# Each SwiGLU of a two-layer encoder in two halves of its columns, each half with its own part of the down projection

## The chip, the cores and the metric

The kernel runs on one core of one Trainium2 chip. The metric is the device time of one execution in microseconds (us); the median of several runs is compared. Engines are PE (matmuls), PEld (its weight loads), DVE, ACT, POOL and SP (which issues the DMAs).

## The reference, cut to what matters

The input is 256 tokens of width 1024. Two layers each add a SwiGLU, a mixer and another SwiGLU to the running sum x, each on RMS-normalised x. The mixer of layer 0 is grouped attention, that of layer 1 neighbourhood attention; the change does not touch them.

```
def swiglu(h, w_gate, w_up, w_down):
    return (jax.nn.silu(h @ w_gate) * (h @ w_up)) @ w_down
...
    for layer in range(DEPTH):
        i = layer // 2
        h = rms_norm(x, ffn1_norm[layer])
        x = x + 0.5 * swiglu(h, ffn1_w_gate[layer], ffn1_w_up[layer], ffn1_w_down[layer])
        h = rms_norm(x, mix_norm[layer])
...
        h = rms_norm(x, ffn2_norm[layer])
        x = x + 0.5 * swiglu(h, ffn2_w_gate[layer], ffn2_w_up[layer], ffn2_w_down[layer])
    return rms_norm(x, final_norm)
```

The inner width D_FF is 2816, that is 22 blocks of 128 rows of w_down, or 11 pairs of blocks. All data is float32.

## The kernel before

**Stages.** The program runs six stages in a row: SwiGLU (stage 0), even mixer (1), SwiGLU (2), SwiGLU (3), odd mixer (4), SwiGLU (5). x lies in two tiles of 128 tokens, `x0` and `x1`.

**Products.** Each float32 operand is split into a high and a low part: ACT copies the high part (`high_part`, tiles `hi`), DVE subtracts it to get the low part (`low_part`, tiles `lo`). A product is three matmuls (`mm`, lines 407 to 409): high by high, low by high, high by low. Weights arrive by DMA in raw tiles of 1 MB (three buffers, `RAWS`), are split into pieces of 512 columns, two pieces to a split of 1024, and wait in seven buffers (`FIT["wp"]`). One piece serves both token tiles, so six matmuls.

**A SwiGLU stage (`ffn`).** The 2816 columns of gate and up are done in six chunks (`FF_CHUNKS`). For each chunk the gate of both token tiles is accumulated in two s banks of PSUM, then the up part in two pj banks; ACT applies silu, DVE multiplies (`glu`), PE transposes the product, and it is split again (tiles `g`). After all six chunks comes the down projection over the 11 pairs of blocks. `DOWN` lists for each stage in which order, and how: `p` is a plain pair (two blocks, two token tiles, two halves of the output: eight products), `s` a Strassen pair. A Strassen pair (`seven`) needs seven products instead of eight, and for it DVE forms sums of the weights (line 338) and of the activations (`quarters`, `sums_of`), which are split too (tiles `shi`, `slo`; `FIT["sum"]` buffers).

**Banks.** PSUM has eight banks, handed out by tags in turn: three s, two pj, one o, two tp. A down uses all of them: four for the output `Y`, four for the Strassen sums `M`.

**End of a stage.** Once the last Strassen pair is issued, `combine` adds the four sums `M` into x (one ACT copy, line 713, and eight DVE operations, lines 710 to 728). The last two pairs of the list (`HELD`) are held back and run output half by output half, so that each half of x can be added (`add_to_x`, line 537) while PE goes on. Then PE transposes x for the next stage (`prepare`, line 462), ACT and DVE split it (lines 447 and 452).

**Order.** Every engine runs its instructions in the order in which the program writes them. The code decides that order with a clock of its own: each product calls `tick`, which moves the waiting tasks (the generators) one step on, and supplies the next split when the rate set for the place (`RATE`, `DOWN_RATE`, `ENDS`) makes it due.

Of the kernel before, what the change touches and what calls it, by code (L numbers as in the profile page):

```python
# [30 lines left out]
FF_CHUNKS = [512, 512, 512, 512, 384, 384]  # L31
# [17 lines left out]
HELD = 2  # L49
# [106 lines left out]
def pairs(stage):  # L156
    return [({"p": "plain", "s": "strassen"}[o[0]], int(o[1:])) for o in DOWN[stage].split()]
# [9 lines left out]
class Trunk:  # L167
# [4 lines left out]
    def __init__(self, ctx, tc, a, out):  # L172
        self.ctx, self.tc, self.nc, self.a, self.out = ctx, tc, tc.nc, a, out
        pool = lambda name, bufs, **kw: ctx.enter_context(tc.tile_pool(name=name, bufs=bufs, **kw))
        self.one = pool("one", 1)
        self.ph = None
        self.raw = pool("raw", RAWS)
        self.wp = pool("wp", FIT["wp"])

        self.two = pool("two", 2)  # L180
        self.acc = pool("acc", 1, space=PSUM)
        self.n = 0
        self.rate = RATE[0]
# [69 lines left out]
    def plan(self):  # L253
# [288 lines left out]
    def first_gates(self, W):  # L542
# [26 lines left out]
        self.due = -AHEAD_START * RATE[0]  # L569
# [11 lines left out]
    def ffn(self):  # L581
        nc = self.nc
        self.rate = RATE[self.now.n]

        gT = [{}, {}]
        down = pairs(self.now.n)
        tasks = []

        paired = {2 * pair: [] for kind, pair in down if kind == "strassen"}
        sums = {}  # L590

# [4 lines left out]
        def glu(tt, f0, w, u, s):  # L596
# [7 lines left out]
            pairs = [f for f in range(f0, f0 + n) if f in paired and f + 1 < f0 + n]  # L604
            parts = []
            for f in pairs:
                yield from quarters(tt, f, tb, f - f0)

            if tt == 1 and f0 + n - 2 in pairs:
# [4 lines left out]
            for f in pairs if tt == 1 else []:  # L614
                yield from sums_of(f)

        def quarters(tt, f, tb, at):

            block = lambda i: tb[:, (at + i) * P : (at + i + 1) * P]
            if tt == 0:  # L620
                paired[f] = self.t([P, 4, P], "quarters")
# [10 lines left out]
        def sums_of(f):  # L632
# [5 lines left out]
            hi, lo = (self.t([P, 4, P], f"k{f}{p}", 1, F32R) for p in "hl")  # L638
# [6 lines left out]
        for ci, w in enumerate(FF_CHUNKS):  # L645
            G = self.take(KD)
            S = []
            if self.now.n + ci == 0:
                both = self.first_gates(G)
            for tt in range(NT):  # L650
                g = both[tt] if self.now.n + ci == 0 else self.project(self.ready(tt), G, "s")
                S.append(self.t([P, 512], "silu", 2))
                self.start(silu(tt, w, g, S[tt]))
            U = self.take(KD)
            for tt in range(NT):
                u = self.project(self.now.hT[tt], U, "pj")
                tasks.append(self.start(glu(tt, f0, w, u, S[tt])))
            f0 += w // P
# [3 lines left out]
        if self.next.n == 6:  # L662
# [3 lines left out]
        Y = [[self.bank(("o", "pj")[i] if tt == 0 else "s") for i in range(2)] for tt in range(NT)]  # L666
# [13 lines left out]
        M = {}  # L680

        def seven(pair, first, last):
            b11, b21, b22, t7, t5, t8, t6 = self.take(7)
            if first:
                for task in tasks:
                    self.finish(task)
                self.rate = DOWN_RATE[self.now.n]
# [4 lines left out]
            def temp(name, tag, lh, piece):  # L692
                if first:
# [53 lines left out]
        if self.next.n == 6:
            last = [self.t([P, 2, 512], "shi", FIT["sum"], F32R) for _ in range(NT)]
            self.last = [t.bitcast(F32).rearrange("p a w -> p (a w)") for t in last]
        held = [f for _, pair in down[-HELD:] for f in (2 * pair, 2 * pair + 1)]  # L750
        for f in held:
            W[f] = self.take(2)
        for tt in range(NT):
            for sl in parts[tt]:
# [4 lines left out]
                self.start(self.add_to_x(tt, sl, Y[tt][sl.start // 512] if to is None else to, 0.5))  # L759
# [564 lines left out]
```

## Time and profile before

| | |
|---|---|
| three runs | 965.45, 966.27, 966.73 us (median 966.27) |
| the profiled execution: its time, its span | 965.2 us, 963.4 us |
| PE, DVE, ACT, POOL busy | 99%, 72%, 58%, 9% of the span |
| mean granted PE clock | 0.998 of full speed |
| bytes moved by DMA | 171.64 MB, 178 GB/s on average |

The span reaches from the first to the last instruction; the profiled execution's own time is 1.8 us longer. Busy times overlap, so their sum is more than the span. PE's ends are modelled, so its busy share says that it had work, not how fast it did it.

### The profile page before, as it was taken

How to read it: one execution, taken by the hardware profiler on the slowest of the kernel's cores; microseconds unless marked ns; L12 is line 12 of the kernel's file. 1: busy time of each engine (PE TensorE's matmuls, PEld its weight loads, DVE VectorE, ACT ScalarE, POOL GpSimd, SP SyncE). 2: the span in 40 equal slices, each digit the busy share in tenths (PEclk: the TensorE clock that was granted, in tenths of full speed). 3: DMA queues.
4: the chain of work that ended last, by engine and by line, in shares of the span. 5: the costliest groups of instructions: out<-in, count | busy, mean ns of one | idle time of the engine just before them, and what ended most of it. 6: DMA issues, size and time to landing. Idle time of an engine off the chain costs nothing.

```text
span 963.4 us, 12838 instructions
## 1 busy us (share of the span) xinstructions
PE 950.2 (99%) x4803; PEld 803.6 (83%) x4803; DVE 696.2 (72%) x1104; ACT 557.4 (58%) x965; POOL 87.5 (9%) x152
## 2 busy tenths in 40 slices
PE   9999999999999999999999999999999999999997
PEld 6888998877878888988888899888878888889886
DVE  6665679778866655797865558789877676656987
ACT  7554556477776555565554455547877576545551
POOL 1020000063410000000000000005130000000002
PEclk9999999999999999999999999999999999999999
DMA  8565555644426744666456556564624366545651
GB/s 293 196 237 177 184 209 180 214 132 100 120 88 212 226 153 133 239 219 218 143 195 205 172 156 231 194 227 134 197 101 146 118 206 196 195 147 175 220 172 67
DMA packets 82367, 171.64 MB, mean 178 GB/s; under 512 B 3712, under 2 KB 25216, under 8 KB 82304
## 3 DMA queue, kind: packets, MB, share of 16 engines
q1 hardware_dynamic: 81728, 170.23, 53.5%
q8 instruction: 37, 0.61, 0.3%
q10 hardware_dynamic: 576, 0.59, 0.2%
q14 instruction: 26, 0.21, 0.1%
HBM read 169.76 MB, written 1.05 MB: 177 GB/s over the span
## 4 chain that ended last, share of the span: by engine, by line
PE 91%; DVE 4%; ACT 2%; POOL 1%; issue 1%; DMA 1%; POOLq 0%; ACTq 0%; DVEq 0%
PE pj L407 14%; PE pj L409 14%; PE pj L408 14%; PE s L407 12%; PE s L409 12%; PE s L408 11%; PE tp L484 3%; PE o L815 2%; PE o L409 1%; PE o L407 1%; PE o L408 1%; PE tp L894 1%; DVE lo L418 1%; PE tp L462 1%; PE s L830 1%
## 5 line engine op out<-in xcount | busy, mean ns | idle before, releaser
L418 DVE TENSOR_TENSOR lo<-raw,hi 128x1024 fp32r<-128x1024 f32 (+2 forms) x388 | 383.7, 1012 | 122.0 <-ACT hi L415 118.5
L415 ACT ACTIVATE hi<-raw 128x1024 fp32r<-128x1024 f32 (+2 forms) x388 | 328.1, 878 | 151.0 <-PE pj L409 101.6
L407 PE MATMUL pj<-hi,th 128*128 128x512 f32 (+1 forms) x512 | 198.1, 387 | 0.0
L409 PE MATMUL pj<-hi,tl 128*128 128x512 f32 (+1 forms) x512 | 192.9, 377 | 0.0
L408 PE MATMUL pj<-lo,th 128*128 128x512 f32 (+1 forms) x512 | 192.7, 376 | 0.1
L407 PE MATMUL s<-hi,th 128*128 128x512 f32 (+1 forms) x400 | 152.1, 380 | 0.0
L409 PE MATMUL s<-hi,tl 128*128 128x512 f32 (+1 forms) x400 | 149.1, 373 | 0.0
L408 PE MATMUL s<-lo,th 128*128 128x512 f32 (+1 forms) x400 | 148.9, 372 | 0.0
L409 PEld LDWEIGHTS pj<-hi,tl 128*128 128x128 f32 x512 | 96.1, 188 | 15.5
L407 PEld LDWEIGHTS pj<-hi,th 128*128 128x128 f32 x512 | 96.4, 188 | 13.8 <-issue 0.9
L408 PEld LDWEIGHTS pj<-lo,th 128*128 128x128 f32 x512 | 96.4, 188 | 13.4 <-DVE lo L418 0.5
L409 PEld LDWEIGHTS s<-hi,tl 128*128 128x128 f32 x400 | 75.2, 188 | 11.0
L408 PEld LDWEIGHTS s<-lo,th 128*128 128x128 f32 x400 | 75.3, 188 | 10.3
L407 PEld LDWEIGHTS s<-hi,th 128*128 128x128 f32 x400 | 75.3, 188 | 10.1
L599 DVE SCALAR_TENSOR_TENSOR glu<-pj,rstd,silu 128x512 f32<-128x512 f32 (+1 forms) x48 | 33.6, 701 | 36.8 <-PE pj L409 36.6
L418 DVE TENSOR_TENSOR g_l<-tp,g_h 128x384 fp32r<-128x384 f32 (+1 forms) x48 | 29.0, 604 | 21.8 <-ACT g_h L415 21.8
L427 POOL TENSOR_TENSOR rstd<-var,mhalf 128x1 f32<-128x1 f32 (+2 forms) x16 | 15.2, 948 | 311.0 <-DVE var L425 310.9
L407 PE MATMUL s<-hi,g_h 128*128 128x512 f32 (+1 forms) x108 | 42.8, 396 | 0.0
L415 ACT ACTIVATE g_h<-tp 128x384 fp32r<-128x384 f32 (+1 forms) x48 | 25.2, 526 | 29.1 <-PE tp L484 19.0
L409 PE MATMUL s<-hi,g_l 128*128 128x512 f32 (+1 forms) x108 | 42.0, 389 | 0.0
L408 PE MATMUL s<-lo,g_h 128*128 128x512 f32 (+1 forms) x108 | 41.9, 388 | 0.0
L447 ACT ACTIVATE th<-tp,mats 128x128 fp32r<-128x128 f32 x88 | 25.1, 371 | 28.3 <-PE tp L462 26.1
(378 smaller groups left out, 1380.7 us busy)
## 6 DMA issues: line engine op xcount, KB each, us to landing
raw<-in_ffn_w_down SPq DMA_DIRECT2D x44, 1024.0 KB, 5.1
raw<-in_ffn_w_up SPq DMA_DIRECT2D x32, 1024.0 KB, 5.4
raw<-in_ffn_w_gate SPq DMA_DIRECT2D x30, 1024.0 KB, 5.2
raw<-in_ffn_w_gate SPq DMA_DIRECT2D x16, 768.0 KB, 4.4
raw<-in_ffn_w_up SPq DMA_DIRECT2D x16, 768.0 KB, 4.6
raw<-in_odd_w_qkv SPq DMA_DIRECT2D x12, 1024.0 KB, 5.4
raw<-in_even_w_in SPq DMA_DIRECT2D x4, 1024.0 KB, 5.2
raw<-in_even_w_out SPq DMA_DIRECT2D x8, 512.0 KB, 5.7
```

What stands on the lines that cost most here:

```text
L407: mm(ps, h, wh, start=first, stop=False)
L408: mm(ps, h, wl, start=False, stop=False)
L409: mm(ps, l, wh, start=False, stop=last)
L415: self.nc.scalar.activation(hi, src, AF.Copy)
L418: self.nc.vector.tensor_tensor(lo, src, hi.bitcast(F32), op=ALU.subtract)
L427: nc.gpsimd.tensor_tensor(r[:, :n], v[:, :n], self.mhalf[:, :n], op=ALU.pow)
L447: self.nc.scalar.activation(hi, tb[:, j * P : j * P + P], AF.Copy, scale=gain)
L462: nc.tensor.transpose(tb[:, j * P : (j + 1) * P], self.x[tt][:, b * P : (b + 1) * P], self.ident)
L484: self.nc.tensor.transpose(tb[:, i * P : (i + 1) * P], src[:, i * P : (i + 1) * P], self.ident)
L599: nc.vector.scalar_tensor_tensor(m[:, :w], u[:, :w], self.now.r[tt], s[:, :w], op0=ALU.mult, op1=ALU.mult)
L815: self.nc.tensor.matmul(O[64 * s : 64 * s + 64, i * P : i * P + P], v(b0 + i, s, kc), pT[s][:, i, kc, :], start=(kc == 0), stop=(kc == 1),)
L830: nc.tensor.matmul(S[:, i, :], q, kz[s], start=True, stop=False)
```

## The change

The six chunks are put into two halves (`HALVES`) of three. Each half does gate and up of its three chunks and then its part of the down projection: pairs 0 to 5 in the first half, 6 to 10 in the second. The down projection becomes a method of its own (`down`) that runs twice per stage, each time with a combine and with adds into x; only the second starts the work for the next stage. One pair is held in the first half, two in the second. The sets of `DOWN` are written anew, with 14 letters s in place of 17. The buffers of the Strassen splits go from three to five, the tiles `g` are shared by both halves, and output and sums change the tags of their banks. The rates are written anew.

```diff
-FF_CHUNKS = [512, 512, 512, 512, 384, 384]
...
+HALVES = [[512, 512, 512], [512, 384, 384]]
...
-    0: "p0 s1 p2 s3 p4 s5 p6 s7 p8 p9 p10",
-    2: "p0 s1 p2 s3 p5 p4 s7 p10 s8 p6 p9",
-    3: "p0 s1 p2 s3 s5 p4 p7 p10 s8 p6 p9",
-    5: "p0 s1 p2 s3 s5 p4 s7 s8 p10 p6 p9",
+    0: ["p1 p3 s2 s5 p0 p4", "p6 s7 p8 p10 p9"],
+    2: ["p0 p2 s1 s5 p4 p3", "p6 s7 s8 p10 p9"],
+    3: ["p0 s1 p2 s5 p4 p3", "p6 s7 s8 p10 p9"],
+    5: ["p1 p2 s5 p4 p3 p0", "p6 s7 s8 p10 p9"],
...
-FIT = {"wp": 7, "sum": 3}
+FIT = {"wp": 7, "sum": 5}
...
-RATE = {0: 0.58, 2: 0.58, 3: 0.53, 5: 0.63}
-DOWN_RATE = {0: 1.22, 2: 1.2, 3: 1.2, 5: 1.2}
-ENDS = {0: [0.42, 0], 2: [0.3, 1], 3: [0.35, 0], 5: [0.4, 0]}
+RATE = {0: [0.55, 0.75], 2: [0.65, 0.47], 3: [0.6, 0.5], 5: [0.6, 0.47]}
+DOWN_RATE = {0: [1.18, 1.2], 2: [1.25, 1.1], 3: [1.2, 1.2], 5: [1.3, 1.2]}
+ENDS = {0: [[0.4, 0], [0.4, 0]], 2: [[0.38, 3], [0.4, 0]], 3: [[0.38, -1], [0.4, -1]], 5: [[0.48, 0], [0.4, -1]]}
...
-HELD = 2
+HELD = [1, 2]
...
-            for w in FF_CHUNKS:
-                first = stage == 0 and c0 == 0
-                yield from columns(a[n + "_w_gate"][l], [(c0, w)], FIRST if first else None, "narrow" if first else "wide")
-                yield from columns(a[n + "_w_up"][l], [(c0, w)], None, "wide")
-                c0 += w
-            for i, (kind, pair) in enumerate(pairs(stage)):
-                src = a[n + "_w_down"][l][2 * pair * P : 2 * (pair + 1) * P, :].rearrange("(k p) n -> p k n", p=P)
-                uses = [2, 3 if stage == 5 and i >= len(pairs(stage)) - HELD else 2]
-                yield [(slice(0, P), src)], 2, D, uses, "wide" if kind == "plain" else kind
+            for half, chunks in enumerate(HALVES):
+                for w in chunks:
...
+                    yield from columns(
+                        a[n + "_w_gate"][l], [(c0, w)], FIRST if first else None, "narrow" if first else "wide"
+                    )
+                    yield from columns(a[n + "_w_up"][l], [(c0, w)], None, "wide")
+                    c0 += w
+                down = pairs(stage, half)
+                for i, (kind, pair) in enumerate(down):
+                    src = a[n + "_w_down"][l][2 * pair * P : 2 * (pair + 1) * P, :].rearrange("(k p) n -> p k n", p=P)
+                    uses = [2, 3 if stage == 5 and half == 1 and i >= len(down) - HELD[half] else 2]
+                    yield [(slice(0, P), src)], 2, D, uses, "wide" if kind == "plain" else kind
...
+    def split_psum(self, tb, n, tag, dest, fit=None):
+        hi, lo = (self.t([P, fit or n, P], f"{tag}{p}", 1, F32R)[:, :n, :] for p in "hl")
         flat = lambda t: t.rearrange("p a b -> p (a b)")
...
-        if nxt.n < 6:
+        if nxt.n < 6 or not last:
             yield 1
         x = self.x[tt][:, sl.start : sl.start + ps.shape[-1]]
         self.nc.vector.scalar_tensor_tensor(x, ps, scale, x, op0=ALU.mult, op1=ALU.add)
...
-        self.rate = RATE[self.now.n]
...
-            yield from self.split_psum(tb, n, f"g{tt}_{f0}_", parts)
+            yield from self.split_psum(tb, n, f"g{tt}_{ci}_", parts, 4)
...
         f0 = 0
-        for ci, w in enumerate(FF_CHUNKS):
-            G = self.take(KD)
-            S = []
-            if self.now.n + ci == 0:
-                both = self.first_gates(G)
-            for tt in range(NT):
-                g = both[tt] if self.now.n + ci == 0 else self.project(self.ready(tt), G, "s")
-                S.append(self.t([P, 512], "silu", 2))
-                self.start(silu(tt, w, g, S[tt]))
...
+        for half, chunks in enumerate(HALVES):
+            self.rate = RATE[self.now.n][half]
+            for ci, w in enumerate(chunks):
+                G = self.take(KD)
+                S = []
+                if self.now.n + f0 == 0:
+                    both = self.first_gates(G)
+                for tt in range(NT):
+                    g = both[tt] if self.now.n + f0 == 0 else self.project(self.ready(tt), G, "s")
+                    S.append(self.t([P, 512], "silu", 2))
+                    self.start(silu(tt, w, g, S[tt]))
+                U = self.take(KD)
+                for tt in range(NT):
+                    u = self.project(self.now.hT[tt], U, "pj")
+                    tasks.append(self.start(glu(tt, ci, f0, w, u, S[tt])))
+                f0 += w // P
+            self.down(half, gT, sums, tasks)
+
+    def down(self, half, gT, sums, tasks):
...
+        down, kept = pairs(self.now.n, half), HELD[half]
...
+        end = self.next.n == 6 and half == 1
         W = {}
 
         parts = [[slice(0, 512), slice(512, 1024)] for _ in range(NT)]
-        if self.next.n == 6:
+        if end:
...
-        Y = [[self.bank(("o", "pj")[i] if tt == 0 else "s") for i in range(2)] for tt in range(NT)]
+        M = {"5": self.bank("s")}
+        Y = [[self.bank("s" if tt == 0 else ("o", "pj")[i]) for i in range(2)] for tt in range(NT)]
...
             def temp(name, tag, lh, piece):
-                if first:
+                if name not in M:
                     M[name] = self.bank(tag)
                 self.mm(M[name], lh, piece, first, last)
...
-        for i, (kind, pair) in enumerate(down[:-HELD]):
+        for i, (kind, pair) in enumerate(down[:-kept]):
             if kind == "strassen":
                 seven(pair, i == order[0], i == order[-1])
                 if i == order[-1]:
                     self.start(combine())
-                    self.rate, self.due = ENDS[self.now.n]
+                    self.rate, self.due = ENDS[self.now.n][half]
                 continue
...
-        held = [f for _, pair in down[-HELD:] for f in (2 * pair, 2 * pair + 1)]
+        held = [f for _, pair in down[-kept:] for f in (2 * pair, 2 * pair + 1)]
         for f in held:
             W[f] = self.take(2)
...
                 for f in held:
                     use(f, tt, sl, f == held[-1], to)
-                self.start(self.add_to_x(tt, sl, Y[tt][sl.start // 512] if to is None else to, 0.5))
+                self.start(self.add_to_x(tt, sl, Y[tt][sl.start // 512] if to is None else to, 0.5, half == 1))
```

On PE the old order has 4371 rows and the new one 4380; on DVE 1061 and 1081, on ACT 829 and 818, on SP 192 and 192.

The first place is in stage 0 on PE, at the end of chunk 2's up and the start of chunk 3's gate. Before, the up (pj_762) is followed at once by the gate of the next chunk (s_811):

```order
L407 MATMUL pj_762<-hi_707,th_265 128x512
L408 MATMUL pj_762<-lo_708,th_265 128x512
L409 MATMUL pj_762<-hi_707,tl_266 128x512
L407 MATMUL s_811<-hi_728,th_120 128x512
L408 MATMUL s_811<-lo_729,th_120 128x512
L409 MATMUL s_811<-hi_728,tl_121 128x512
```

Now the last matmuls of the first half's down (pj_810, fourth part of the output) stand ahead of that gate, which is called s_1067:

```order
L412 MATMUL pj_810<-hi_960,g_2_h_852 128x512
L413 MATMUL pj_810<-lo_961,g_2_h_852 128x512
L414 MATMUL pj_810<-hi_960,g_2_l_853 128x512
L412 MATMUL s_1067<-hi_969,th_120 128x512
L413 MATMUL s_1067<-lo_970,th_120 128x512
L414 MATMUL s_1067<-hi_969,tl_121 128x512
```

The whole first down (pairs p1 p3 s2 s5 p0 p4) has moved between chunk 2 and chunk 3. The new gate's bank is the one that held the Strassen sum s_806.

The second place is the same point on DVE. Before, there are only splits of weights (lo) and the products of gate and up (glu):

```order
L418 TENSOR_TENSOR lo_729<-raw_528,hi_728 128x1024
L418 TENSOR_TENSOR lo_742<-raw_528,hi_741 128x1024
L418 TENSOR_TENSOR lo_760<-raw_562,hi_759 128x1024
L599 SCALAR_TENSOR_TENSOR glu_767<-pj_721,rstd_239,silu_676 128x512
L418 TENSOR_TENSOR lo_776<-raw_562,hi_775 128x1024
```

Now the combine (lines 722 to 740) and the adds into x (541) are there, with splits for the coming gate between them (x_85 is x0, x_86 is x1):

```order
L423 TENSOR_TENSOR lo_980<-raw_749,hi_979 128x1024
L726 SCALAR_TENSOR_TENSOR x_85<-pj_903,x_85 128x512
L729 SCALAR_TENSOR_TENSOR silu_995<-tp_940,silu_989 128x512
L732 SCALAR_TENSOR_TENSOR glu_1000<-tp_920,silu_995 128x512
L735 SCALAR_TENSOR_TENSOR silu_1005<-s_806,silu_995 128x512
L722 TENSOR_TENSOR x_85<-x_85,silu_1005 128x512
L423 TENSOR_TENSOR lo_1015<-raw_785,hi_1014 128x1024
L740 SCALAR_TENSOR_TENSOR glu_1011<-s_806,glu_1000 128x512
L722 TENSOR_TENSOR x_86<-x_86,glu_1000 128x512
L722 TENSOR_TENSOR x_86<-x_86,glu_1011 128x512
L423 TENSOR_TENSOR lo_1037<-raw_785,hi_1036 128x1024
L541 SCALAR_TENSOR_TENSOR x_85<-s_807,x_85 128x512
```

The last reader of the bank of s_806 is L740; ahead of it stand five rows of the combine and one split, and the five splits lo_931 to lo_970 and the one shown first come before these.

The third place is the end of stage 3 on DVE, between the first and the second add into x0. Before:

```order
L710 TENSOR_TENSOR x_85<-x_85,silu_6148 128x512
L537 SCALAR_TENSOR_TENSOR x_85<-o_5761,x_85 128x512
L728 SCALAR_TENSOR_TENSOR glu_6154<-s_5841,glu_6143 128x512
L710 TENSOR_TENSOR x_86<-x_86,glu_6143 128x512
L710 TENSOR_TENSOR x_86<-x_86,glu_6154 128x512
L537 SCALAR_TENSOR_TENSOR x_85<-pj_5762,x_85 128x512
```

Now:

```order
L722 TENSOR_TENSOR x_85<-x_85,silu_6199 128x512
L541 SCALAR_TENSOR_TENSOR x_85<-s_6041,x_85 128x512
L423 TENSOR_TENSOR lo_6210<-raw_5973,hi_6209 128x512
L740 SCALAR_TENSOR_TENSOR glu_6205<-s_6040,glu_6194 128x512
L722 TENSOR_TENSOR x_86<-x_86,glu_6194 128x512
L722 TENSOR_TENSOR x_86<-x_86,glu_6205 128x512
L423 TENSOR_TENSOR lo_6210<-raw_5973,hi_6209 128x512
L541 SCALAR_TENSOR_TENSOR x_85<-s_6042,x_85 128x512
```

Two splits of 512 columns have come in ahead of the second add. In stage 2 one split of 1024 has come in at the same place.

## Rows read from the trace of the kernel before

**Rows 1.** The page's first lines: span, and busy us (share of the span) xinstructions.

```profile
span 963.4 us, 12838 instructions
PE 950.2 (99%) x4803; PEld 803.6 (83%) x4803; DVE 696.2 (72%) x1104; ACT 557.4 (58%) x965; POOL 87.5 (9%) x152
```

**Rows 2.** Busy time by stretch: stage 2's down and gate/up, even and odd mixer.

```profile
core 0: us, PE busy (x) PEld busy (x) DVE busy (x) ACT busy (x) POOL busy (x), PEclk, DMA share, GB/s
415.00:470.00 55.00, 55.00 (x248) 45.52 (x247) 45.63 (x53) 29.41 (x39) 0.00 (x0) 1.00 0.56 198
288.00:378.00 90.00, 90.00 (x417) 74.91 (x416) 55.48 (x69) 49.43 (x69) 0.55 (x1) 1.00 0.58 187
195.00:288.00 93.00, 89.67 (x558) 71.39 (x557) 74.00 (x178) 68.42 (x186) 40.20 (x79) 1.00 0.40 111
655.00:776.00 121.00, 120.10 (x699) 98.30 (x698) 94.57 (x242) 86.75 (x202) 26.18 (x28) 1.00 0.45 147
```

**Rows 3.** Timeline of PE in stage 2's down: start us, us, what; ten matmuls.

```profile
439.92 0.39 PE L407 MATMUL pj<-hi,g_h 128*128 128x512 f32 x1
440.14 0.39 PE L408 MATMUL pj<-lo,g_h 128*128 128x512 f32 x1
...
441.73 0.39 PE L409 MATMUL s<-hi,g_l 128*128 128x512 f32 x1
441.96 0.39 PE L407 MATMUL pj<-hi,g_h 128*128 128x512 f32 x1
```

**Rows 4.** Groups of PE's matmuls by form, whole span: busy us, mean ns.

```profile
L407 PE MATMUL s<-shi,g_h 128*128 128x512 f32 x17 | 6.6, 389 | 0.0
```

**Rows 5.** Timeline of DVE at the end of stage 3.

```profile
643.79 0.68 DVE L714 SCALAR_TENSOR_TENSOR x<-pj,x 128x512 f32<-128x512 f32 x1
...
646.43 0.69 DVE L710 TENSOR_TENSOR x<-x,silu 128x512 f32<-128x512 f32 x1
647.04 0.68 DVE L537 SCALAR_TENSOR_TENSOR x<-o,x 128x512 f32<-128x512 f32 x1
647.64 0.68 DVE L728 SCALAR_TENSOR_TENSOR glu<-s,glu 128x512 f32<-128x512 f32 x1
648.24 1.28 DVE L710 TENSOR_TENSOR x<-x,glu 128x512 f32<-128x512 f32 x2
649.44 0.68 DVE L537 SCALAR_TENSOR_TENSOR x<-pj,x 128x512 f32<-128x512 f32 x1
```

**Rows 6.** Groups of DVE by form, whole span: busy us, mean ns, idle before.

```profile
L418 DVE TENSOR_TENSOR lo<-raw,hi 128x1024 fp32r<-128x1024 f32 x195 | 232.9, 1223 | 73.3 <-ACT hi L415 71.2
L418 DVE TENSOR_TENSOR lo<-raw,hi 128x512 fp32r<-128x512 f32 x129 | 91.2, 723 | 17.5 <-ACT hi L415 16.8
...
L338 DVE TENSOR_TENSOR two<-raw 128x1024 f32<-128x1024 f32 x17 | 20.7, 1218 | 0.0
L338 DVE TENSOR_TENSOR raw<-two,raw 128x512 f32<-128x512 f32 x17 | 11.8, 692 | 0.6
```

**Rows 7.** Timeline of PE at the end of stage 3.

```profile
641.35 0.39 PE L409 MATMUL tp<-shi,k16l 128*128 128x512 f32 x1
...
648.38 0.60 PE L462 MATMUL tp<-mats,x 128*128 128x128 f32 x4
...
651.60 0.60 PE L462 MATMUL tp<-mats,x 128*128 128x128 f32 x4
```

**Rows 8.** Timeline of ACT at the end of stage 3; in brackets its wait.

```profile
641.91 1.15 ACT L415 ACTIVATE hi<-raw 128x512 fp32r<-128x512 f32 x2 [1.33 <-DMA raw<-in_odd_w_qkv]
642.97 0.58 ACT L713 ACTIVATE silu<-pj 128x512 f32<-128x512 f32 x1
```

**Rows 9.** Timeline at the end of the program.

```profile
956.35 0.28 PE L409 MATMUL tp<-hi,g_l 128*128 128x128 f32 x1
...
959.42 0.36 SPq L1203 DMA_DIRECT2D out<-shi  x1
```

More of the change, by code (lines that the diff above doesn't have):

```diff
@@ L153, in constants, with pairs @@
     }
-def pairs(stage):
-    return [({"p": "plain", "s": "strassen"}[o[0]], int(o[1:])) for o in DOWN[stage].split()]
+def pairs(stage, half):
+    return [({"p": "plain", "s": "strassen"}[o[0]], int(o[1:])) for o in DOWN[stage][half].split()]
 class Stage:
@@ L182, in __init__ @@
         self.n = 0
-        self.rate = RATE[0]
+        self.rate = RATE[0][0]
         self.tasks, self.last, self.last_v, self.late = [], [], [EPS] * NT, []
@@ L271, in ffn @@
             c0 = 0
[L272 to L280 removed]
+            for half, chunks in enumerate(HALVES):
+                for w in chunks:
+                    first = stage == 0 and c0 == 0
+                    yield from columns(
[8 more added lines that the diff above has]
+                    yield [(slice(0, P), src)], 2, D, uses, "wide" if kind == "plain" else kind
         def even():
@@ L568, in first_gates @@
             self.warm()
-        self.due = -AHEAD_START * RATE[0]
+        self.due = -AHEAD_START * RATE[0][0]
         for tt in range(NT):
@@ L582, in ffn @@
         nc = self.nc
-        self.rate = RATE[self.now.n]
         gT = [{}, {}]
-        down = pairs(self.now.n)
         tasks = []
-        paired = {2 * pair: [] for kind, pair in down if kind == "strassen"}
+        paired = {2 * pair: [] for half in range(2) for kind, pair in pairs(self.now.n, half) if kind == "strassen"}
         sums = {}
+        place = {2 * pair: n for half in range(2) for n, pair in enumerate(sorted(p for kind, p in pairs(self.now.n, half) if kind == "strassen"))}
         def silu(tt, w, g, s):
@@ L603, in glu @@
             yield 1
-            pairs = [f for f in range(f0, f0 + n) if f in paired and f + 1 < f0 + n]
+            both = [f for f in range(f0, f0 + n) if f in paired and f + 1 < f0 + n]
             parts = []
-            for f in pairs:
+            for f in both:
                 yield from quarters(tt, f, tb, f - f0)
-            if tt == 1 and f0 + n - 2 in pairs:
+            if tt == 1 and f0 + n - 2 in both:
                 n -= 1
-            yield from self.split_psum(tb, n, f"g{tt}_{f0}_", parts)
+            yield from self.split_psum(tb, n, f"g{tt}_{ci}_", parts, 4)
             for j, part in enumerate(parts):
                 gT[tt][f0 + j] = part
-            for f in pairs if tt == 1 else []:
+            for f in both if tt == 1 else []:
                 yield from sums_of(f)
@@ L637, in sums_of @@
             yield 1
-            hi, lo = (self.t([P, 4, P], f"k{f}{p}", 1, F32R) for p in "hl")
+            hi, lo = (self.t([P, 4, P], f"k{place[f]}{p}", 1, F32R) for p in "hl")
             self.high_part(hi, k)
@@ L644, in ffn @@
         f0 = 0
-        for ci, w in enumerate(FF_CHUNKS):
-            G = self.take(KD)
-            S = []
-            if self.now.n + ci == 0:
-                both = self.first_gates(G)
-            for tt in range(NT):
-                g = both[tt] if self.now.n + ci == 0 else self.project(self.ready(tt), G, "s")
-                S.append(self.t([P, 512], "silu", 2))
-                self.start(silu(tt, w, g, S[tt]))
[L654 to L658, printed above, removed]
+        for half, chunks in enumerate(HALVES):
[16 more added lines that the diff above has]
+    def down(self, half, gT, sums, tasks):
+        nc = self.nc
+        down, kept = pairs(self.now.n, half), HELD[half]
+        end = self.next.n == 6 and half == 1
         W = {}
         parts = [[slice(0, 512), slice(512, 1024)] for _ in range(NT)]
-        if self.next.n == 6:
+        if end:
             self.last_gain = self.t([P, D], "last_gain")
@@ L686, in seven @@
                     self.finish(task)
-                self.rate = DOWN_RATE[self.now.n]
+                self.rate = DOWN_RATE[self.now.n][half]
             f = 2 * pair
@@ L744, in ffn @@
                 for tt in range(NT):
-                    for half in range(2):
-                        use(f, tt, slice(half * 512, half * 512 + 512))
-        if self.next.n == 6:
+                    for nh in range(2):
+                        use(f, tt, slice(nh * 512, nh * 512 + 512))
+        if end:
             last = [self.t([P, 2, 512], "shi", FIT["sum"], F32R) for _ in range(NT)]
             self.last = [t.bitcast(F32).rearrange("p a w -> p (a w)") for t in last]
-        held = [f for _, pair in down[-HELD:] for f in (2 * pair, 2 * pair + 1)]
+        held = [f for _, pair in down[-kept:] for f in (2 * pair, 2 * pair + 1)]
         for f in held:
```

8 lines of the change are left out of this document (2 added, 6 removed).

## The prediction

> **What bounds the kernel now.** I read the page's first part, then the busy time by stretch, then the PE timeline, and last the DVE and ACT timelines at one stage end. The page says that PE is busy for 950.2 of 963.4 us, DVE for 72% [rows 1]. That alone would not decide, since a busy PE need not be a PE at its peak; the stretches do. In a gate and up stretch PE is busy for 90.00 of 90.00 us, with DVE at 55.48 and ACT at 49.43; in a down stretch for 55.00 of 55.00, with DVE at 45.63 [rows 2]. PE has idle time inside the program only in the two mixers, 93.00 - 89.67 = 3.33 us and 121.00 - 120.10 = 0.90 us, besides the loading at the start and the tail [rows 2]. Inside a dense stretch matmuls of 512 columns start at a fixed step: nine steps lie between 439.92 and 441.96 us, 2.04 us, 0.227 us each [rows 3]. The granted clock is 1.00 in all these rows, so it is the upper of the two levels (2.4 GHz). So in the SwiGLU stages time is the number of matmuls times 0.227 us, and nothing that only relieves DVE, ACT or the DMA can shorten them. The change touches only these stages; the mixers keep their code.
>
> **The change part by part.** *Matmuls.* A plain pair of rows of the down weights takes 2 x 2 x 2 products of three matmuls, 24; a Strassen pair takes seven products, 21. The group of matmuls that multiplies one piece of each Strassen pair has 17 members [rows 4], and the old table has 4 + 4 + 4 + 5 = 17 letters s. The new one has 3 + 4 + 4 + 3 = 14 (stage 0 loses one, stage 5 two). Three pairs become plain: 3 x 3 = 9 more matmuls, which is also the difference of PE's rows in the two orders (4371 and 4380). Gate and up keep the same six chunks, and the transposes stay as many. By rows 3 nine matmuls cost 9 x 0.227 = **2.04 us**, and as PE has no idle time there, all of it is on the path. The Trainium skill, TensorE: Matmul & The Clock Gate, section Back-to-back issue gap, gives another price: about 216 ns for an isolated warm matmul of 512 columns, and 131 ns for a stream of weight load and matmul pairs. By these nine would cost 1.94 or 1.18 us; the trace agrees with neither, its step being 11 ns above the first.
>
> *DVE and ACT.* Each stage now ends two downs, so each has a second combine (eight DVE operations and one ACT copy of 512 columns) and four more adds into x. At 0.68 to 0.69 us [rows 5] that is 12 x 0.69 = 8.3 us of DVE per stage, 33 us in all. Against it, each Strassen pair made plain takes away a 1.22 us sum, two half-size ones, and the extra splits [rows 6]. This lies under PE: in a stage DVE is free for 34.5 of 90 us in gate and up, and 9.4 of 55 us in down [rows 2]. Were there no cover it would cost tens of us; there is. The DMAs are as many as before (192 rows on SP in both orders), and the 16 engines are 56 to 58% busy in these stretches [rows 2], so that down weights now come between gate weights costs nothing. POOL does nothing more.
>
> *The half boundary.* This is new: after the first half's last product the next gate begins, and its first output takes an s bank that held a Strassen sum (s_806 in the order). The last reader of that bank is the combine's eighth DVE row, L740. What stands behind that wait on PE is the whole queue. The cover is what PE has left after the last Strassen pair: two plain pairs in stages 0, 2 and 3, 48 x 0.227 = 10.9 us, and three in stage 5, 16.3 us. What DVE must do meanwhile, at most, if it has run ahead of PE by nothing, is seven splits of 1024 at 1.22 us [rows 6] and six combine operations at 0.69 [rows 5], 12.7 us: 1.8 us late. The nearest row for how it goes is the same combine at the end of stage 3: the last Strassen matmul starts at 641.35 [rows 7] and ends 0.39 later, and the last reader of the bank ends at 647.64 + 0.68 = 648.32 [rows 5]. That is 6.6 us, in which 1.3 us of ACT's wait for weights that had not landed is included [rows 8]. At the boundary one split of 1.22 us is put in and one x add (0.68) left out: 7.1 us, 3.8 us before it is needed. I take 0 of 0 to 1.8 us, three times.
>
> *The stage end.* Here PE transposes x right after the adds into it. At the end of stage 3 the first add ends at 647.04 + 0.68 = 647.72 and its transposes start at 648.38: 0.66 us to spare; the second ends at 650.12 and is read at 651.60: 1.48 to spare [rows 5, 7]. The new order puts two splits of 512 before the second add (lo_6210 in the order), 2 x 0.72 = 1.44 us by their mean [rows 6]. That uses the margin up but for 0.04. Before the first add nothing is put in. The split also waits for ACT's hi, and ACT at this place has been waiting for weights from the DMA [rows 8], so it can come late by itself. In stage 2 one split of 1024 (1.22 us) comes in at the same place, within such a margin. Stage 0 keeps its order, and at the program's end the adds keep their place behind the same held matmuls, so the tail (959.42 to the end) [rows 9] stays. Bounds for all of this: 0, and 1.44 us at each of the two adds of stage 3, 2.9. A gain is excluded, since PE waits for nothing there now. I take 0.3, nearer the lower end, as the margin is used up but not overrun.
>
> *The sum.* 2.04 + 0 + 0.3 = 2.34 us. The profiled execution took 965.2 us, 1.8 us around its span; after the change I expect about 967.5 there. The median of the three runs is 966.27, 1.1 above the profiled one, and with the same addition it becomes **968.6 us**. That is 0.24%, just past the 0.2% (1.93 us) that a measurement of this kernel can tell from no change; its three runs lie 1.3 us apart.
>
> **The rivals.** *A wait at the half boundaries* (slower by more). DVE reaches L740 late because two Strassen pairs in a row (stages 2 and 3) leave it no lead. Against it stands the 6.6 us in the rows, for it the 83% DVE load of the down stretch. It decides once the combine takes over 10.9 us after the last product. Fully out it is 3 x 1.8 = 5.4 us, 974 us; a third of that, 970.4. The Trainium skill speaks for this side: Trainium Kernel Development and Optimization, Best Practices, warns of PSUM pressure, and says that consistent bubbles can mean that SBUF or PSUM ran out. No bubble of that kind is in this trace, though a down holds all eight banks; it ends with the mixer or with x to be made ready, not with a gate that needs a bank at once.
>
> *Faster: the mixers give their idle time back.* With fewer Strassen pairs late in the stages, splits could run ahead and the mixers start with full buffers. There are 3.33 + 0.90 = 4.23 us of PE idle time in them [rows 2]. To be faster by over 0.2% it must give back 2.04 + 1.93 = 3.97 of it, almost all: 964.3 us. Against it: the waits there come from the mixers' own chains (rotary, softmax, transposes), which the change leaves, and the seven buffers of splits and three of raw weights are as many.
>
> *The same mechanism, in part* (no change to be told): 0.5 to 3.9 us come back from the mixers, 964.7 to 968.1, say 967.0. *A cheaper matmul*: an inserted matmul overlaps its neighbours more than the old ones do, and costs between nothing and the step; with half of it, nine cost 1.02 us and the time is 967.6 with the stage end's 0.3. The fixed step in rows 3 speaks against it. The 131 ns of the page on TensorE in the Trainium skill would come out in this way. That the change does not do what it says I exclude, as the orders show the gate of chunk 3 behind a finished down.
>
> **How the numbers follow.** The forecast has 0.55, and of that 0.06 falls within 0.2% by the spread of runs. The half boundary has 0.13, the mixers in full 0.06, in part 0.22, the cheaper matmul 0.04. Slower by over 0.2%: 0.49 + 0.13 = 0.62. Within: 0.06 + 0.22 + 0.04 = 0.32. Faster: 0.06. The forecast's own range, 2.04 us without any wait to 2.04 + 2.9 at the stage end, is 968.3 to 971.2. The range for 8 in 10 goes down to 966.5, which leaves out the mixers in full (0.06) and the larger give-backs (0.09 of their 0.22, as a small one is likelier), and up to 971.5, which takes in the boundary's smaller waits and leaves out some 0.05.
>
> **What would show it right or wrong.** Right: PE's step stays 0.227 us; stage 5 is longer by six matmuls (1.36 us) and stage 0 by three (0.68); PE is busy throughout every half boundary; the gates' DVE load rises. The boundary's price is shown by a gap of PE ahead of the gate of chunk 3, put down to DVE's L740; the stage end's by a gap ahead of the transposes of x at the end of stage 3, put down to the add L541. The prediction is wrong if PE's idle time in the mixers falls by over 2 us, if the boundaries show gaps of a us each, or if the step of the matmuls differs in plain pairs.

## The result, and the profile after

The changed kernel takes 968.97 us (median of seven runs, 967.91 to 969.6), the kernel before 966.13 us (seven runs beside it, 965.45 to 966.73). The ratio is 1.0029, with a 95% interval of 1.002 to 1.0038: 0.29% slower, 1.9 to 3.7 us. 968.6 was predicted, in a range of 966.5 to 971.5. The profiled execution took 967.91 us with a span of 966.1 us, 2.7 us more than before.

The page's first lines of the changed kernel [rows 1], then PE's group by form [rows 4]:

```profile
PE 952.4 (99%) x4812; PEld 805.1 (83%) x4812; DVE 709.7 (73%) x1125; ACT 551.0 (57%) x954; POOL 87.3 (9%) x152
```

```profile
L412 PE MATMUL o<-shi,g_h 128*128 128x512 f32 x14 | 5.4, 389 | 0.0
```

17 Strassen pairs have become 14, and PE has nine matmuls more (4812 for 4803) and 2.2 us more of busy time. DVE grew by 13.5 us.

Busy time by stretch, with the columns of [rows 2]: 20 us around the half boundaries of stages 0, 2, 3 and 5, then the even mixer.

```profile
95.00:115.00 20.00, 20.00 (x90) 16.57 (x89) 17.34 (x21) 8.21 (x9) 0.00 (x0) 1.00 0.69 240
370.00:390.00 20.00, 20.00 (x90) 16.54 (x89) 16.62 (x21) 7.84 (x9) 0.00 (x0) 1.00 0.71 243
555.00:575.00 20.00, 20.00 (x89) 16.52 (x88) 14.63 (x20) 7.59 (x9) 0.00 (x0) 1.00 0.67 229
862.00:882.00 20.00, 20.00 (x90) 16.57 (x89) 14.50 (x19) 6.91 (x8) 0.00 (x0) 1.00 0.54 179
195.00:288.00 93.00, 90.27 (x562) 71.99 (x561) 74.80 (x179) 69.20 (x188) 39.22 (x79) 1.00 0.41 113
```

PE is busy throughout at every half boundary. The even mixer has 2.73 us of PE idle time where it had 3.33. In the view of PE's waits in that stretch one row differs; first the kernel before, then the changed one (us in total, times, longest):

```profile
PE tp L970 <- POOL kra L923: 1.0, 1, 1.0
```

```profile
PE tp L982 <- POOL kra L935: 0.3, 1, 0.3
```

The boundary of stage 2 itself, on DVE, ACT and PE (timelines of the changed kernel):

```profile
374.36 2.36 DVE L423 TENSOR_TENSOR lo<-raw,hi 128x1024 fp32r<-128x1024 f32 x2 [1.90 <-ACT hi L420]
378.17 1.23 DVE L423 TENSOR_TENSOR lo<-raw,hi 128x1024 fp32r<-128x1024 f32 x1 [1.44 <-ACT hi L420]
379.31 0.68 DVE L726 SCALAR_TENSOR_TENSOR x<-pj,x 128x512 f32<-128x512 f32 x1
...
383.57 0.68 DVE L740 SCALAR_TENSOR_TENSOR glu<-s,glu 128x512 f32<-128x512 f32 x1
```

```profile
377.07 1.06 ACT L420 ACTIVATE hi<-raw 128x1024 fp32r<-128x1024 f32 x1 [1.80 <-DMA raw<-in_ffn_w_gate]
```

```profile
373.48 0.39 PE L414 MATMUL tp<-shi,k1l 128*128 128x512 f32 x1
...
383.23 0.39 PE L412 MATMUL pj<-hi,g_h 128*128 128x512 f32 x1
...
384.59 0.40 PE L412 MATMUL s<-hi,th 128*128 128x512 f32 x1
```

The gate of chunk 3 starts at 384.59, on its step (six steps from 383.23 are 1.36 us, 0.227 each). But the last reader of the Strassen sum's bank, L740, ended at 384.25, 10.4 us after the last Strassen matmul's end (373.48 + 0.39). 0.34 us were to spare, not the 3.8 that the prediction worked out. In the row that it went by, the end of stage 3 in the kernel before, two splits of 512 columns (1.2 us) and 0.8 us of DVE's waiting lay between the product and the combine:

```profile
642.58 1.29 DVE L418 TENSOR_TENSOR lo<-raw,hi 128x512 fp32r<-128x512 f32 x2 [1.03 <-ACT hi L415]
```

Here the combine, at 379.31, is queued behind three splits of 1024 columns (3.5 us) and 1.9 us of DVE's waiting for high parts; ACT stood 1.80 us before the last of these, because gate weights had not landed. At the boundaries of stages 0, 2, 3 and 5 L740 ended 8.1, 10.4, 10.4 and 9.0 us after the product, with 2.7, 0.34, 0.30 and 7.1 us to spare before the gate.

The end of stage 3 [rows 5, 7], where the order has changed, on DVE and PE of the changed kernel:

```profile
650.95 0.68 DVE L541 SCALAR_TENSOR_TENSOR x<-s,x 128x512 f32<-128x512 f32 x1
```

```profile
651.74 0.61 PE L467 MATMUL tp<-mats,x 128*128 128x128 f32 x4
```

The second add ends at 651.63, 0.11 us before it is read, where 1.48 us lay between them.

The end of the program, on DVE, POOL and PE of the changed kernel [rows 9]:

```profile
946.82 0.69 DVE L729 SCALAR_TENSOR_TENSOR silu<-tp,silu 128x512 f32<-128x512 f32 x1 [0.81 <-PE tp L414]
...
949.54 0.69 DVE L541 SCALAR_TENSOR_TENSOR x<-s,x 128x512 f32<-128x512 f32 x1 [0.71 <-PE s L414]
...
950.89 1.76 DVE L722 TENSOR_TENSOR x<-x,silu 128x512 f32<-128x512 f32 x1
...
956.90 0.59 DVE L1213 TENSOR_SCALAR shi<-shi,r 128x704 f32<-128x704 f32 x1 [0.45 <-POOL r L1198]
957.40 0.68 DVE L541 SCALAR_TENSOR_TENSOR x<-o,x 128x512 f32<-128x512 f32 x1
...
961.86 0.59 DVE L1213 TENSOR_SCALAR shi<-shi,r 128x704 f32<-128x704 f32 x1 [0.24 <-POOL r L1198]
```

```profile
950.37 1.74 POOL L1204 TENSOR_TENSOR shi<-x,last_gain 128x512 f32<-128x512 f32 x1 [166.77 <-DVE x L541]
```

```profile
958.07 0.28 PE L414 MATMUL tp<-hi,g_l 128*128 128x128 f32 x1
```

The same two DVE operations in the kernel before, whose last matmul starts at 956.35 [rows 9]:

```profile
954.33 0.68 DVE L537 SCALAR_TENSOR_TENSOR x<-s,x 128x512 f32<-128x512 f32 x1
...
958.81 0.59 DVE L1201 TENSOR_SCALAR shi<-shi,r 128x704 f32<-128x704 f32 x1 [0.24 <-POOL r L1186]
```

So PE's last matmul came 1.72 us later, and DVE's last scaling 3.05 us later: 3.05 us after the last matmul before, 4.38 us after it now. The output's DMA then ended the span 4.0 us later before and 3.65 now. The 2.7 us are 1.72 + 1.33 - 0.35. The last two parts are not in the prediction's sum.

One thing must be taken off when last matmuls of several kernels are compared: the start. One matmul of the up part of chunk 0 serves as a mark; behind it the next weight load waits 0.52 us for a low part in every run. It starts at 22.39 us in the profile of before and at 22.46 after, but at 22.6 to 23.9 in other runs with the same code up to there. In the PE and PEld timelines of the changed kernel:

```profile
22.46 0.39 PE L412 MATMUL pj<-hi,th 128*128 128x512 f32 x1
```

```profile
22.95 0.19 PEld L413 LDWEIGHTS pj<-lo,th 128*128 128x128 f32 x1 [0.52 <-DVE lo L423]
```

What differs is the clock of the first matmuls. In experiment 4, which has the latest mark (23.86), eight steps in a row take 0.43 us each:

```profile
7.92 0.63 PE L413 MATMUL s<-lo,th 128*128 128x512 f32 x1
...
11.33 0.40 PE L412 MATMUL s<-hi,th 128*128 128x512 f32 x1
```

That is the step that experiment 4 shows later at a granted clock of 0.50. Its trace's first record of the granted clock, of 1.00, begins at 11.32 us; in the kernel before it begins at 8.17, and the steps are 0.23 us from 8.25 on. (The view by stretch prints 1.00 for the time ahead of the first record too.) Over all ten kernels the mark comes 0.47 us later for each us by which that record begins later, within 0.1 us.

**Below, "net" is the start of the last matmul less that mark**: 933.96 before, 935.61 after, 1.65 more. "Tail" is from the last matmul's start to the end of DVE's last scaling: 3.05 and 4.38. Nets differ too from one execution to the next: experiment 7, whose code is the changed kernel's up to the end of the program, has 936.04, 0.43 more.

### The profile page after: what moved, and what is told of

Its sections match the earlier page's. It is cut to its first block, busy times and chain, and to the rows that moved or that the text cites. A ratio compares the mean times of both kernels' runs of the same rounds, so it can differ in the third digit from the quotient of the medians.

```text
span 966.1 us, 12910 instructions
## 1 busy us (share of the span) xinstructions
PE 952.4 (99%) x4812; PEld 805.1 (83%) x4812; DVE 709.7 (73%) x1125; ACT 551.0 (57%) x954; POOL 87.3 (9%) x152
## 4 chain that ended last, share of the span: by engine, by line
PE 93%; DVE 2%; ACT 2%; POOL 1%; issue 1%; DMA 0%; POOLq 0%; ACTq 0%; DVEq 0%
PE pj L412 14%; PE pj L414 14%; PE pj L413 14%; PE s L412 12%; PE s L414 12%; PE s L413 12%; PE tp L489 3%; PE o L414 2%; PE o L413 2%; PE o L412 2%; PE o L827 2%; PE tp L906 1%; PE tp L467 1%; PE s L842 1%; PE s L843 1%
## 5 line engine op out<-in xcount | busy, mean ns | idle before, releaser
L412 PEld LDWEIGHTS s<-hi,th 128*128 128x128 f32 x400 | 75.4, 188 | 10.4
L413 PEld LDWEIGHTS s<-lo,th 128*128 128x128 f32 x400 | 75.3, 188 | 10.4
L602 DVE SCALAR_TENSOR_TENSOR glu<-pj,rstd,silu 128x512 f32<-128x512 f32 (+1 forms) x48 | 33.7, 701 | 31.1 <-PE pj L414 30.8
L414 PE MATMUL s<-hi,g_l 128*128 128x512 f32 x134 | 52.2, 390 | 0.0
L413 PE MATMUL s<-lo,g_h 128*128 128x512 f32 x134 | 52.2, 389 | 0.0
L412 PE MATMUL s<-hi,g_h 128*128 128x512 f32 x134 | 52.2, 389 | 0.0
L597 ACT ACTIVATE silu<-s,rstd 128x512 f32<-128x512 f32 (+1 forms) x48 | 31.2, 650 | 35.7 <-PE s L414 34.2
```

The lines of the kernel that those rows point to most:

```text
L412: mm(ps, h, wh, start=first, stop=False)
L413: mm(ps, h, wl, start=False, stop=False)
L414: mm(ps, l, wh, start=False, stop=last)
L597: nc.scalar.activation(s[:, :w], g[:, :w], AF.Silu, scale=self.rstd_of(tt))
L602: nc.vector.scalar_tensor_tensor(m[:, :w], u[:, :w], self.now.r[tt], s[:, :w], op0=ALU.mult, op1=ALU.mult)
```

## The experiments

Ratios are to the kernel before, run beside them: 965.93 us for the first four, 965.85 for the last four.

**1. Only the nine matmuls.** The kernel before, with 14 Strassen pairs:

```diff
-    0: "p0 s1 p2 s3 p4 s5 p6 s7 p8 p9 p10",
+    0: "p0 s1 p2 s3 p4 s5 p6 p7 p8 p9 p10",
-    5: "p0 s1 p2 s3 s5 p4 s7 s8 p10 p6 p9",
+    5: "p0 s1 p2 p3 p5 p4 s7 s8 p10 p6 p9",
```

> The kernel before, with one whole down per layer, but only 14 Strassen pairs: pair 7 of stage 0 and pairs 3 and 5 of stage 5 become plain. Theory (the matmuls are the price): nine matmuls more at the step of 0.227 us move the start of the last matmul from 956.35 to 956.35 + 2.04 = 958.39 us; the end of stage 5 keeps its order, so the stretch from there to the end of the span stays 7.07 us; time 966.13 + 2.04 = 968.2 us. Rival (the halving itself is the price, through its second combines and adds): no halving here, so 966.1 us. Rival (a matmul in a plain pair costs half a step): 967.2 us.

966.97 us, ratio 1.0011 (1.0002 to 1.002). The last matmul starts at 958.63, net 935.95, 1.99 us more than before: a matmul costs its full step, and the rival of half a step falls. But the time rose by only 1.04 us. The tail is 2.64 us, 0.41 shorter: DVE's combine began 12.15 us ahead of the last matmul, where it had been 11.75. Most of the rest is the output's DMA, 3.6 us here. So the theory was right on PE and wrong in taking the tail as fixed.

**2. Only the order at the end.** The kernel before with the end of the new list:

```diff
-    5: "p0 s1 p2 s3 s5 p4 s7 s8 p10 p6 p9",
+    5: "p0 s1 p2 s3 s5 p4 p6 s7 s8 p10 p9",
```

> The kernel before with its 17 Strassen pairs, one whole down per layer, but the pairs of stage 5 end as in the changed kernel: the plain pair that stood between the last Strassen pair and the two held pairs goes ahead, so that the combine has only the held pairs over it. Theory (the longer tail comes from the combine's place): last matmul starts at 956.35 as before, the stretch from there to the end grows from 7.07 to about 8.0 us, time 966.13 + 0.96 = 967.1 us. Rival (the longer tail comes from the halving, by its other banks for the sums or by its second half's adds): tail 7.07 and 966.1 us.

967.75 us, ratio 1.0017 (1.0009 to 1.0026). Net 933.90, as before; tail 4.89. Its DVE timeline:

```profile
950.88 1.77 DVE L710 TENSOR_TENSOR x<-x,silu 128x512 f32<-128x512 f32 x1
...
961.87 0.59 DVE L1201 TENSOR_SCALAR shi<-shi,r 128x704 f32<-128x704 f32 x1 [0.24 <-POOL r L1186]
```

It is the picture of the changed kernel, without any halving. With no plain pair between the last product and the held ones, the combine and the adds of the held parts fall on DVE at the same time. The mechanism is shown; its size is larger: the tail grew by 1.84 us (1.33 in the changed kernel), and the stretch to the end of the span by 1.7 for an expected 0.96.

**3. The order at the end, given back by one plain pair.** In the changed kernel:

```diff
-    5: ["p1 p2 s5 p4 p3 p0", "p6 s7 s8 p10 p9"],
+    5: ["p1 p2 s5 p4 p3 p0", "p6 s7 p8 p10 p9"],
```

> The changed kernel, with pair 8 of stage 5 plain: 13 Strassen pairs, and a plain pair of 24 matmuls stands again between the last Strassen pair and the held ones. Theory: three matmuls more, last matmul starts at 958.07 + 0.68 = 958.75 us, but the tail falls from 8.03 back to about 7.1 us; time 968.97 + 0.68 - 0.96 = 968.7 us. Rival (the tail has nothing to do with the combine): tail 8.0 us, time 968.97 + 0.68 = 969.65 us.

967.43 us, ratio 1.0015 (1.0006 to 1.0024): three matmuls more, and faster than the changed kernel. Net 936.34, 0.73 more, as expected; tail 2.50, so it fell by 1.88 and not by 0.96. On DVE the adds now wait for PE:

```profile
950.92 0.69 DVE L541 SCALAR_TENSOR_TENSOR x<-s,x 128x512 f32<-128x512 f32 x1 [2.03 <-PE s L414]
...
953.64 0.69 DVE L541 SCALAR_TENSOR_TENSOR x<-s,x 128x512 f32<-128x512 f32 x1 [1.30 <-PE s L414]
...
961.35 0.59 DVE L1213 TENSOR_SCALAR shi<-shi,r 128x704 f32<-128x704 f32 x1 [0.24 <-POOL r L1198]
```

**4. Halving with 17 Strassen pairs.**

```diff
-    0: ["p1 p3 s2 s5 p0 p4", "p6 s7 p8 p10 p9"],
+    0: ["p1 p3 s2 s5 p0 p4", "p6 s7 s8 p10 p9"],
-    5: ["p1 p2 s5 p4 p3 p0", "p6 s7 s8 p10 p9"],
+    5: ["p0 s1 s3 s5 p2 p4", "p6 s7 s8 p10 p9"],
```

> The changed kernel with 17 Strassen pairs as before: pair 8 of stage 0 and pairs 1 and 3 of stage 5 become Strassen again, always with two plain pairs behind the last one of a first half. Matmuls as many as in the kernel before, so this is the halving alone. Theory (PE's matmuls and the tail are all of the price): last matmul starts 2.04 us earlier than in the changed kernel, at 956.03 us, tail 8.0 us, time 968.97 - 2.04 = 966.9 us. Rival (a half is too short to carry the work of so many Strassen pairs): gaps of PE of some us show in stage 5 ahead of or at the first half's end, or at the end of stage 0, and the time is at or over 969 us.

971.88 us, ratio 1.0065 (1.0053 to 1.0078), with as many matmuls as before. The rival holds: net 940.07, 6.5 us over the theory's 933.57. PE's timeline and its busy time by stretch:

```profile
172.70 0.55 PE L489 MATMUL tp<-mats,glu 128*128 128x128 f32 x3 [1.27 <-DVE glu L602]
...
878.41 0.76 PE L412 MATMUL s<-hi,th 128*128 128x512 f32 x1 [2.35 <-DVE glu L740]
...
881.85 0.40 PE L414 MATMUL s<-hi,tl 128*128 128x512 f32 x1
```

```profile
875.00:878.40 3.40, 1.06 (x5) 0.58 (x4) 3.37 (x6) 2.12 (x2) 0.00 (x0) 0.99 0.24 94
878.40:880.00 1.60, 1.59 (x4) 1.31 (x5) 1.60 (x3) 0.00 (x0) 0.00 (x0) 0.50 0.68 144
```

Here is the wait that the prediction's first rival named: PE stands 2.35 us at the gate of chunk 3 for L740, behind two whole plain pairs. After it the granted clock is 0.50, the lower of its two levels (1.2 GHz), and the eight steps from 878.41 to 881.85 take 3.44 us instead of 1.82: another 1.6 us. At the end of stage 0 PE waits 1.27 us for the product of up and silu (L602) of the last chunk, and in stage 5 0.57 us for the same line. These four are 5.8 of the 6.5 us. So a half does not carry as many Strassen pairs as the whole did, at least at the changed kernel's rates: rates set anew for 17 pairs were not tried.

**5. Half the cover at the boundary.** In the changed kernel, stages 2 and 3:

```diff
-    2: ["p0 p2 s1 s5 p4 p3", "p6 s7 s8 p10 p9"],
-    3: ["p0 s1 p2 s5 p4 p3", "p6 s7 s8 p10 p9"],
+    2: ["p0 p2 p4 s1 s5 p3", "p6 s7 s8 p10 p9"],
+    3: ["p0 p4 p2 s1 s5 p3", "p6 s7 s8 p10 p9"],
```

> The changed kernel with as many Strassen pairs, but in the first halves of stages 2 and 3 the last Strassen pair stands one pair later, so that one plain pair (24 matmuls, 5.4 us) instead of two (10.9 us) lies between it and the gate of chunk 3. Reading of the changed kernel's trace: there the last reader of the bank ended some 10.6 us after the last Strassen product began (stage 2) and the gate came 0.3 us later. If that is how long DVE takes, PE now waits about 5 us ahead of the gate at each of the two boundaries, and the time is near 968.97 + 10 = 979 us. By the prediction's 7.1 us it waits 1.7 us each, 972.4 us. Rival (the boundary has no price, as DVE reaches the bank soon after the product): 969.0 us.

973.21 us, ratio 1.007 (1.0057 to 1.0082). The time lies near one of the three, but none of them holds: at the boundary almost nothing happens; DVE and PE in stage 2:

```profile
386.32 0.68 DVE L541 SCALAR_TENSOR_TENSOR x<-s,x 128x512 f32<-128x512 f32 x1
...
389.04 0.68 DVE L740 SCALAR_TENSOR_TENSOR glu<-s,glu 128x512 f32<-128x512 f32 x1
```

```profile
386.83 0.39 PE L414 MATMUL pj<-hi,g_l 128*128 128x512 f32 x1
387.15 0.47 PE L412 MATMUL s<-hi,th 128*128 128x512 f32 x1
```

The gate starts at 387.15, long before L740 has run and right after the add L541 has ended at 387.00: it cannot have the bank that L740 reads, and its start fits the output's that L541 has just read. So the wait for L740 is not fixed to the gate. The time went elsewhere: in three downs PE waits for 0.9, 1.0 and 1.3 us ahead of the transposes of the last chunk's product. One of them, on PE and DVE:

```profile
359.32 0.66 PE L489 MATMUL tp<-mats,glu 128*128 128x128 f32 x4 [0.93 <-DVE glu L602]
```

```profile
355.93 1.22 DVE L343 TENSOR_TENSOR two<-raw 128x1024 f32<-128x1024 f32 x1
357.18 0.69 DVE L343 TENSOR_TENSOR raw<-two,raw 128x512 f32<-128x512 f32 x1
357.91 0.69 DVE L343 TENSOR_TENSOR raw<-raw 128x512 f32<-128x512 f32 x1
358.52 0.74 DVE L602 SCALAR_TENSOR_TENSOR glu<-pj,rstd,silu 128x512 f32<-128x512 f32 x1
```

The three weight sums of a Strassen pair (2.6 us) stand ahead of L602 in DVE's queue, and PE's transposes wait for L602. The 1.27 us in experiment 4 have the same releaser. Net 939.65 is 4.04 us over the changed kernel; these waits are 3.2 of them, the rest was not followed.

**6. The same 14 pairs, one moved.** Pair 8 of stage 5 plain, pair 1 Strassen:

```diff
-    5: ["p1 p2 s5 p4 p3 p0", "p6 s7 s8 p10 p9"],
+    5: ["p0 s1 p2 s5 p4 p3", "p6 s7 p8 p10 p9"],
```

> The changed kernel with its 14 Strassen pairs, one of stage 5 moved: pair 8 plain (a plain pair between the last Strassen pair and the held ones again), pair 1 in the first half Strassen instead. The matmuls stay as many as in the changed kernel, only the combine's cover at the end differs. Theory: last matmul starts at 958.07 us but for the loading at the start, DVE waits for PE at the end as it did in the run with pair 8 plain, and the last scaling ends 2.5 instead of 4.4 us after that matmul; time 967.43 - 0.68 = 966.8 us. Rival (an added Strassen pair in the first half of stage 5 makes DVE late at the boundary): a gap of PE ahead of the gate of chunk 3, 967.5 us or more.

966.69 us as expected, ratio 1.0005 (0.9996 to 1.0014). Net 935.73 (935.61 in the changed kernel), tail 2.50, no gap at the boundary. With the changed kernel's matmuls and the halving, but the combine covered at the end, the kernel cannot be told from the one before, and its interval lies wholly below the changed kernel's (1.002 to 1.0038).

**7. POOL's product taken away** (`after`, first half of x0):

```diff
-            nc.gpsimd.tensor_tensor(self.last[tt][:, sl], x, self.last_gain[:, sl], op=ALU.mult)
+            if tt:
+                nc.gpsimd.tensor_tensor(self.last[tt][:, sl], x, self.last_gain[:, sl], op=ALU.mult)
+            else:
+                self.late.append(sl)
```

> The changed kernel; only POOL's product of the last gain with the first half of x0 is taken from POOL and made on DVE with the second half's, at the end of x0. Theory (DVE's add of x and silu took 1.76 instead of 0.69 us because POOL's product ran at the same time): that add takes 0.69 us again, DVE gains 1.07 and loses one product of 0.69 us, so the end comes 0.4 us earlier: 968.6 us. Rival (the add is slow for another reason, such as waiting for its operand): it stays at 1.76 us, and the end comes 0.7 us later.

967.77 us, ratio 1.0019 (1.001 to 1.0027). Tail 3.58, 0.80 shorter. DVE's timeline:

```profile
951.46 0.69 DVE L722 TENSOR_TENSOR x<-x,silu 128x512 f32<-128x512 f32 x1
...
956.66 0.59 DVE L1216 TENSOR_SCALAR shi<-shi,r 128x704 f32<-128x704 f32 x1
```

The add takes 0.69 us again, so POOL's product was what held it. The gain is twice the 0.4 expected, because the extra product on DVE fills the 0.45 us for which the scaling had waited for POOL's r.

In the kernel before, the two do not meet: the combine's last adds end at 949.73, ahead of POOL's product.

```profile
948.45 1.28 DVE L710 TENSOR_TENSOR x<-x,glu 128x512 f32<-128x512 f32 x2
```

```profile
950.47 1.75 POOL L1192 TENSOR_TENSOR shi<-x,last_gain 128x512 f32<-128x512 f32 x1 [167.23 <-DVE x L537]
```

So of the 1.33 us by which the tail grew, 0.80 go away without this meeting; it comes about because the combine has moved on to the held pairs' adds.

**8. A plain pair ahead of the last Strassen pair, before.**

```diff
-    5: "p0 s1 p2 s3 s5 p4 s7 s8 p10 p6 p9",
+    5: "p0 s1 p2 s3 s5 s7 p4 s8 p10 p6 p9",
```

> The kernel before with its 17 Strassen pairs and one whole down per layer; in stage 5 pair 4 moves from between pairs 5 and 7 to between pairs 7 and 8. Theory (the tail's length is DVE's backlog of splits ahead of the combine): with a plain pair ahead of the last Strassen pair DVE comes to the combine with less behind it, and the last scaling ends 2.5 instead of 3.05 us after the last matmul began; time 965.4 us, faster than both kernels. Rival: the splits before three Strassen pairs in a row come late, and PE waits there; 966 us or more.

965.73 us, ratio 0.9998 (0.9989 to 1.0007): no difference. Net 933.97, so no wait of PE; tail 3.17, no shorter. DVE stood 1.56 us for ACT ahead of the combine (1.37 in the kernel before), which began at 945.06, 11.60 us ahead of the last matmul where it had been 11.75:

```profile
942.79 2.36 DVE L418 TENSOR_TENSOR lo<-raw,hi 128x1024 fp32r<-128x1024 f32 x2 [1.56 <-ACT hi L415]
945.06 0.69 DVE L714 SCALAR_TENSOR_TENSOR x<-pj,x 128x512 f32<-128x512 f32 x1
```

No version was found that beats the kernel before.

## Why the prediction was right, and where it was not

*Matmuls, 2.04 us.* Right: PE's step stayed 0.227 us, and experiment 1, which adds these nine and nothing else, moves the last matmul by 1.99 us. The Trainium skill's 131 ns (TensorE: Matmul & The Clock Gate, section Back-to-back issue gap) would have given 1.18; the trace does not agree with it.

*DVE and ACT, hidden.* Right for the sum: 13.5 us more of DVE lengthened no dense stretch. Wrong at one place, the end of the program, where nothing of PE is left to hide it.

*The half boundary, 0.* The number is right, its working is not. The last reader was to be through 7.1 us after the last product; it took 8.1 to 10.4. The mis-sized term is what stands between the product and the combine: in stage 2 the splits there took 2.3 us more than in the row at the end of stage 3, as they are wider and one more, and the waits for gate weights 1.1 us more. The combine stayed within the cover, by 0.30 us at the least, and experiment 4, with three Strassen pairs in the half, overran it by 2.35 us. The rival was nearer than its chance of 0.13 suggests. It would also have cost more than its wait, through the clock. And the cover is not what decides alone: in experiment 5 half of it did no harm, since there, by its start, the gate took another bank.

*The stage end, 0.3.* The margin is used up as foreseen, to 0.11 us, and no more. Less the mark these transposes start 0.07 us later than before (629.21 in the kernel before, 629.28 now); 0.3 was a little high, by no more than such nets scatter.

*The mixers in part.* This happened, outside the forecast: PE's wait for POOL's `kra` in the even mixer fell from 1.0 to 0.3 us, which gives 0.62 back. It is there in every halved kernel (the step to that transpose is 0.72 to 0.75 us in the changed one and in experiments 3 to 7) and in no other (1.35 to 1.37 in the kernel before and in 1, 2 and 8). POOL's rows from the `rstd` ahead of it to `kra` span 7.2 us before and 6.6 after; why they got shorter was not tried. In the odd mixer 0.2 us were lost.

*The tail stays.* **This step failed.** The prediction said that at the end "the adds keep their place behind the same held matmuls". They do, but the combine does not: in the new list the plain pair that stood between it and the held pairs has gone ahead. DVE's last scaling came 4.38 us after the last matmul instead of 3.05. Experiment 2 makes this by the order alone, 3 and 6 take it away.

From the starts of the same rows less the mark (the transposes of x at each stage's end, and the last matmul), the account for PE is 0.70 (stage 0) - 0.70 (even mixer) + 0.09 (stages 2 and 3) + 0.20 (odd mixer) + 1.36 (stage 5) = 1.65 us, as measured. With 1.33 for the tail it is 2.98, close to the 2.84 between the medians. That the forecast of 2.34 was near is luck in part: a gain and a loss that it left out, -0.70 and +1.33, partly cancel.

## What to carry to other kernels

When a list of work is cut in two, look not only at the new seam but at what each kind of work has behind it afterwards: the same held matmuls hid a combine before and did not after, and one plain pair put in front of them in place of a Strassen pair was worth 1.9 us of tail, more than the 0.68 us that its three extra matmuls cost. A margin read from one place (6.6 us at a stage end) does not carry to another where the splits are wider and other transfers are due.

## What the runs showed of the hardware

- **A POOL operation can hold up a DVE operation.** An add of two tiles in SBUF took 1.76 us instead of 0.69 while POOL multiplied (950.37 to 952.11), and ended 0.54 us after POOL did. With POOL's product gone it took 0.69. The Trainium skill says so (SBUF — State Buffer, section SBUF: two separate sides): a DVE operation with two inputs in SBUF and a POOL operation that reads SBUF exclude each other for a whole instruction. The rows agree, for a DVE operation that comes second: after POOL's end the add took 0.54 us, less than its 0.69 alone.
- **A wait of PE can cost more than itself.** After 2.35 us of idle time the granted clock was 0.50 for some 3.4 us (878.3 to 881.7), which cost 1.6 us more. After 1.27 us, in the same run, it stayed at 1.00.
- **The first matmuls run at the step of the lower clock, for a time that differs between executions.** PE began the first gate at 7.1 to 7.5 us in all ten profiles, and the granted clock's first record, of 1.00, began at 8.17 to 11.32 us; the mark moved with it, from 22.39 to 23.86 us. The output's last DMA took 3.6 to 4.0 us. Differences of under 1 us between single profiles must be taken net of both.
